# A hybrid attention and state-space block: first projections on unscaled, turned tokens

## The chip, the cores and the metric

The kernel runs on one core of a Trainium2 chip. A core has TensorE (matrix products), VectorE, ScalarE and GpSimd, SyncE which issues transfers, and 16 DMA engines. The metric is the device time of one execution in microseconds, as the median of several runs. A profile of one execution gives each instruction's start and duration.

## The reference

One decoder block on 512 tokens and 16 learned meta tokens, 1024 features, all in float32. What matters here:

```python
h = concat([meta, x])                       # 528 tokens
xn = rmsnorm(h, g_mix_pre)                  # h * rsqrt(mean(h*h) + eps) * g
proj = xn @ w_in                            # q, k, v, r, a_low, u, z_gla, z_ssm
log_a = log_sigmoid(a_low @ w_gate_up + b_gate) / 16
o = gla_chunked(q, k, v, log_a)             # gated linear attention, 4 heads
y_gla = (rmsnorm(o) * silu(r)) @ w_o_gla
y_s = s5_ssm(u, ...)                        # complex diagonal state-space layer, 64 groups
glu = gelu(y_s) @ w_glu + b_glu
y_ssm = glu[..., :1024] * sigmoid(glu[..., 1024:])
mixed = sigmoid(z_gla) * y_gla + sigmoid(z_ssm) * y_ssm
h = h + rmsnorm(mixed @ w_out, g_mix_post)
f = square(relu(rmsnorm(h, g_ffn_pre) @ w_ff1)) @ w_ff2
h = h + rmsnorm(f, g_ffn_post)              # output: the 512 tokens
```

Since rmsnorm scales each token by one number, `xn @ w` equals the product of `h * g` with `w`, scaled by that number per token afterwards.

## The kernel before

Every large product is made of three matmuls, because operands are split into a high and a low part: high x high, high x low, low x high (`mm3`). A weight tile is 1024 x 128: it is loaded into `wraw` (three buffers), ScalarE rounds it into `whi` (`split_w_hi`, three buffers), VectorE subtracts to give `wlo` (`split_w_lo`, three buffers). The activations are kept turned, features on the partitions, as `xh` and `xl`, [128, 8, 528]. A tile's product with all 528 tokens is made in two halves (`HALVES`), 256 and 272 columns; each half is 24 matmuls. A z tile is made of 24 matmuls with 512 columns.

The start: four tiles of 128 tokens and the meta tokens are loaded as rows, in `xt`. For each, ScalarE sums the squares (`squared`) and takes a root, VectorE makes the reciprocal root (`rooted`) and the normalised rows `xn` (`normed`), using `gpre`, the gain spread over the partitions by two matmuls with one row. TensorE turns `xn` in blocks of 128 x 128 (`turned_tokens`), ScalarE copies the high part to `xh` (`high`) and VectorE the low part to `xl` (`low`). Between them TensorE multiplies dummy matmuls (`busy`). Meanwhile the first three u tiles are multiplied: first halves as soon as the first 256 tokens are there, second halves behind the last. ScalarE takes each half from the accumulator into `ut` (three buffers) in another order of tokens, and GpSimd's queue stores it to DRAM (`u_out`). In this stage each engine's order is the order of the program text (`InOrder`, `keep_in_program_order`).

Behind it comes `low_rank`, the product with 16 columns of `w_in` that yields `alow`, from `xh`, `xl` and `wa`. Then a list of tiles, `dense`, is worked off by `slot()`, each with the weights of the tile fetched two ahead (`fetch`, `AHEAD = 2`): before S5's blocks, u tiles 3 to 7, four z tiles of `zs` and one of `zg`. Among these, `gate_up(h)` multiplies `alow` with `wgr` (the gate weights, split by `gate_weights` out of `wgu`, which six small loads on GpSimd's queue bring), and `decay_sums` makes the sums of log decays: exp, log and a scan for each head with a mask that restarts it at each 128 tokens. VectorE at the same time makes the state-space layer's parameters (`chain`, `powers`, `chunk_powers`, `b_bar`).

After that, eight blocks of S5, each with several `slot()` calls among its steps so that TensorE has dense work: v, q, k, the remaining z tiles, r tiles, and the o tiles. Then the GLU, the output product and the two feed-forward products. TensorE keeps program order throughout the part shown; on the other engines and queues a scheduler sets the order outside the start, and buffers' reuse adds waits.

Of the kernel before, what the change touches and what calls it, by code (L numbers as in the profile page):

```python
# [16 lines left out]
P = 128  # L17
# [3 lines left out]
NM = 16  # L21
# [28 lines left out]
def hybrid_block(ctx: ExitStack, tc: tile.TileContext, io, out: bass.AP):  # L50
# [204 lines left out]
    def u_half(w, ut, q, within=None):  # L255

        a, b = HALVES[q]
        ps = bank("mm")
        feat_tile(w, xh, xl, a, b, ps[:, : b - a], within=within)

        def taken():
            src = ps.rearrange("p (c s) -> p s c", s=T8)
            first = NM // T8 + a // T8
            S.copy(ut[:, :, first : first + 32], src[:, :, :32])
            if q:
                S.copy(ut[:, :, : NM // T8], src[:, :, 32:34])

        return taken
# [9 lines left out]
    gpre = mk(pxt, [P, D], tag="gpre")  # L278
    grow = mk(pxt, [1, D], tag="grow")
    one_row = mk(pxt, [1, P], tag="one_row")  # L280
    V.memset(one_row, 1.0)
    nc.scalar.dma_start(grow, io["g_mix_pre"][0].rearrange("(o d) -> o d", o=1))
    xm = mk(pxt, [P, D], tag="xt", bufs=5)
    xts, raws = [], []
    loaded = nc.sync.dma_start(xm[:NM], io["meta_tokens"])
    ones = mk(pxt, [P, 256], tag="ones")
    V.memset(ones, 1.0)
    idle = bank()

    def busy(n):  # L290

        for _ in range(n):
            PE.matmul(idle[:, :256], ones[:, :P], ones, start=True, stop=True)
# [3 lines left out]

    def x_load(t):
        xt = mk(pxt, [P, D], tag="xt", bufs=5)
        xts.append((xt, P, t * P))  # L300
        return nc.sync.dma_start(xt, io["x"][0, t * P : (t + 1) * P, :])


    for kind, i in (("x", 0), ("x", 1), ("u", 0), ("x", 2), ("u", 1), ("x", 3), ("u", 2)):
        with behind():
            if kind == "x":
                loaded = x_load(i)
            else:
                loaded, raw = raw_w(w_in[:, C_U + i * P : C_U + (i + 1) * P])
                raws.append(raw)  # L310
    xts.append((xm, NM, SEQ))
# [3 lines left out]
    nc.gpsimd.dma_start(vecs, io["vecs"])  # L315
    V, S = InOrder(nc.vector), InOrder(nc.scalar)
    ss = mk(pxt, [P, 5], tag="xss")
    rs = mk(pxt, [P, 5], tag="xrs")
    xns = {}

    def squared(i):
        xt, n, _ = xts[i]
        sq = mk(pxt, [P, D], tag="xsq", bufs=1)
        S.activation(sq[:n], xt[:n], AF.Square, accum_out=ss[:n, i : i + 1])

    def rooted(i):

        n = xts[i][1]
        y, ssum = rs[:n, i : i + 1], ss[:n, i : i + 1]
        parts = mk(pxt, [n, 2], tag="xr_r", bufs=3)  # L330
        a, hm = parts[:, :1], parts[:, 1:]
        S.activation(a, ssum, AF.Sqrt, scale=1.0 / D, bias=epst[:n])
        yield
        V.tensor_scalar(hm, ssum, -0.5 / D, -0.5 * EPS, op0=ALU.mult, op1=ALU.add)
        V.reciprocal(y, a)
        V.scalar_tensor_tensor(a, y, hm, y, op0=ALU.mult, op1=ALU.mult)
        V.scalar_tensor_tensor(y, a, 1.5, y, op0=ALU.add, op1=ALU.mult)

    roots = {}

    def summed(i):
        squared(i)
        roots[i] = rooted(i)
        next(roots[i])

    def normed(i, cols=(0, 512)):
        xt, n, _ = xts[i]
        if i not in xns:
            xns[i] = mk(pxt, [P, D], tag="xn", bufs=3)
            next(roots[i], None)  # L350
        xn = xns[i]
        for c in cols:
            cc = slice(c, c + 512)
            V.scalar_tensor_tensor(xn[:n, cc], xt[:n, cc], rs[:n, i : i + 1], gpre[:n, cc], op0=ALU.mult, op1=ALU.mult)

    def turned(i, tag):
        return [turned_tokens(xns[i][: xts[i][1]], xts[i][1], q, tag if isinstance(tag, str) else tag[q]) for q in range(2)]

    def high(i, q, pvs):
        _, n, col = xts[i]  # L360
        split_hi(xh[:, 4 * q : 4 * q + 4, col : col + n], pvs[q])

    def low(i, q, pvs):
        _, n, col = xts[i]
        dst = slice(4 * q, 4 * q + 4)
        V.tensor_sub(xl[:, dst, col : col + n], pvs[q], f32(xh)[:, dst, col : col + n])

    gps = [bank() for _ in range(2)]
    for i, ps in enumerate(gps):
        PE.matmul(ps, one_row, grow[:, i * 512 : (i + 1) * 512], start=True, stop=True)  # L370
# [12 lines left out]
    w0 = hi0, split_w_lo(raws[0], hi0)
    high(0, 0, t0)
    high(0, 1, t0)
    t1 = turned(1, "sm")
    high(1, 0, t1)
    high(1, 1, t1)
    for q in range(2):
        low(0, q, t0)  # L390
        low(1, q, t1)
    ut0, ut1, ut2 = (u_tile() for _ in range(3))
    take0 = u_half(w0, ut0, 0)
    summed(2)
    hi1 = split_w_hi(raws[1])
    w1 = hi1, split_w_lo(raws[1], hi1)
    take1 = u_half(w1, ut1, 0)
    normed(2)
    summed(3)
    hi2 = split_w_hi(raws[2])  # L400
    w2_ = hi2, split_w_lo(raws[2], hi2)
    take0()
    normed(3)
    ts = {}
    take2 = u_half(w2_, ut2, 0, within=(1, lambda: ts.update({2: turned(2, "mm")})))
    high(2, 0, ts[2])
    high(2, 1, ts[2])
    normed(4, (512,))
    low(2, 0, ts[2])
    low(2, 1, ts[2])  # L410
    t4 = turned(4, "sm")
    t3 = turned(3, ("mm", "sm"))
    take1()
    for q in range(2):
        high(4, q, t4)
        low(4, q, t4)
    for q in range(2):
        high(3, q, t3)
        low(3, q, t3)
    take2()  # L420
    wa = mk(pg, [P, KT, 32], F32R, tag="wa")
    split_hi(wa[:, :, :16], wraw)
    begun = V.tensor_sub(wa[:, :, 16:], wraw, f32(wa)[:, :, :16])
    V, S = nc.vector, nc.scalar
    for blk, w, ut in ((0, w0, ut0), (1, w1, ut1), (2, w2_, ut2)):
        u_half(w, ut, 1)()
        u_out(blk, ut)
# [44 lines left out]

    def gate_up(h):
        for a, b in HALVES:
            ps = bank()[:, : b - a]
            PE.matmul(ps, wgr[:, h * P : (h + 1) * P], alow[:, a:b], start=True, stop=True)
            bg = vecs[:, V_BGATE + h : V_BGATE + h + 1]
            S.activation(ga[:, h, a:b], ps, AF.Abs, bias=bg)
            V.tensor_scalar(mn[:, h, a:b], ps, bg, 0.0, op0=ALU.add, op1=ALU.min)

    def decay_sums():
        S.activation(ga, ga, AF.Exp, scale=-1.0)
        S.activation(ga, ga, AF.Ln, bias=1.0)
        for h in range(HEADS):
            V.tensor_sub(mn[:, h], mn[:, h], ga[:, h])
            b2 = mk(pga, [P, NT], tag="b2", bufs=2)
            V.tensor_tensor_scan(b2, mask01, mn[:, h], 0.0, op0=ALU.mult, op1=ALU.add)
            nc.gpsimd.dma_start(bd[h], b2)
# [21 lines left out]
    def u_slot(m):  # L510
        def go(w):
            ut = u_tile()
            for q in range(2):
                u_half(w, ut, q)()
# [219 lines left out]
    def c_rows():  # L734
        S.activation(CA, CA, AF.Copy, scale=sgn)
        S.activation(CB, CB, AF.Copy, scale=-1.0)
# [27 lines left out]
    with tc.issue_after(begun.ins):  # L764
        fetch(0)
    fetch(1)
# [44 lines left out]
    class Head:  # L811
# [27 lines left out]
        def decays(self):  # L839
# [13 lines left out]
            self.kg = ex([P, NT], dl, "gk", -1.0 / TAU)  # L853
            d1 = mk(pgb, [P, NT], tag="d1")[:, :SEQ]
            V.tensor_sub(d1.rearrange("p (c t) -> p c t", t=CH), bm, bm[:, :, 32:33].to_broadcast([P, 8, CH]))
            self.kin = ex([P, SEQ], d1, "k", -1.0 / TAU)
            self.qin = ex([P, SEQ], d1, "q", 1.0 / TAU)
            dx = mk(pgb, [P, NT], tag="d1")[:, :SEQ].rearrange("p (c t) -> p c t", t=P)
            V.tensor_sub(dx, bp, bp[:, :, 63:64].to_broadcast([P, TT, P]))
            self.kx = ex([P, TT, CH], dx[:, :, :CH], "fk", -1.0 / TAU)  # L860
            self.qx = ex([P, TT, CH], dx[:, :, CH:], "fq", 1.0 / TAU)
            self.dec = ex([P, TT], bp[:, :, P - 1], "dec", 1.0 / TAU)
            self.b2, self.ex = b2, ex

        def query_decay(self):
            self.qg = self.ex([P, SEQ], self.b2[:, :SEQ], "gq", 1.0 / TAU)
# [266 lines left out]
    for kind in ("r0", "r1", "z5", "r2", "r3", "z6", "r4", "r5", "r6", "r7", "z7", *(f"o{m}" for m in range(KT))):  # L1133
# [11 lines left out]
    for b, blk in enumerate(blocks):  # L1145
# [22 lines left out]
        slot()  # L1168
# [20 lines left out]
        slot()  # L1189
# [329 lines left out]
def laid_out(np, given):  # L1519
# [9 lines left out]
    for name, (one, two) in (("b_cols", bt), ("c_cols", ct)):  # L1529
        rows[name] = np.stack([np.concatenate([one, two]), np.concatenate([two, one])])  # L1530
    return {**{name: a[name] for name in _INS}, **rows}


_LAID = ["gla_norm_g", "b_glu", "b_gate", "d_skip", "a_re", "a_im", "log_step", "b_re", "b_im", "c_re", "c_im"]
_INS = [
    "x", "meta_tokens", "g_mix_pre", "w_in", "w_gate_up", "w_o_gla", "w_glu", "w_out", "g_mix_post", "g_ffn_pre", "w_ff1", "w_ff2", "g_ffn_post",
# [21 lines left out]
```

## Time and profile before

| | |
|---|---|
| median of 3 runs | 883.39 us (882.73 to 883.80) |
| the profiled execution | 883.62 us |
| its span | 881.9 us |
| TensorE busy | 869.5 us, 99% of the span |
| VectorE busy | 648.6 us, 74% |
| ScalarE busy | 437.7 us, 50% |
| GpSimd busy | 124.0 us, 14% |
| moved by DMA | 177.36 MB |

The rows of the profile name an engine (PE is TensorE, DVE is VectorE, ACT is ScalarE, POOL is GpSimd, SP is SyncE), the line of the program, the operation, the tile written and the tiles read, and the shape. In a timeline row the first number is the start and the second the duration in us; what stands in brackets is the idle time of that engine just before, and what ended it. In a group's row the total busy time and the mean of one in ns follow the count. TensorE's matmuls are pipelined: a row's duration is longer than the spacing of two starts. In the kernel's start all instructions behind helper `InOrder` carry line L78, and all matmuls L60, so they are told apart by their tiles.

### The profile page before, as it was taken

The numbers are of one execution on the slowest core, as the hardware profiler recorded it, in microseconds if no ns is written. First come the engines' busy times: TensorE is split into PE (matmuls) and PEld (weight loads), VectorE is DVE, ScalarE is ACT, GpSimd is POOL, SyncE is SP. The second block draws the span as 40 slices with busy tenths as digits, with TensorE's granted clock in tenths as the row PEclk, the third lists the DMA queues.
The fourth block names the chain that finished last, engine by engine and source line by source line (L and its number), as shares of the span: only waits on it lengthen the run. The fifth ranks groups of instructions, "written<-read, shape, count | busy, mean of one in ns | idle before, by whom it ended". The sixth has DMA issues, their size and how long they took to land.

```text
span 881.9 us, 13276 instructions
## 1 busy us (share of the span) xinstructions
PE 869.5 (99%) x4856; PEld 742.5 (84%) x4856; DVE 648.6 (74%) x1148; ACT 437.7 (50%) x731; POOL 124.0 (14%) x224
## 2 busy tenths in 40 slices
PE   8999999999999999999999999999999999999996
PEld 6998989898988888888888888988888888888885
DVE  7989898868778698755445765576666678788886
ACT  6475466767655454434333543333222236665763
POOL 1223022030312213232000001021112100000001
PEclk9999999999999999999999999999999999999998
DMA  9647785555454857558545761589998966856564
GB/s 305 179 126 239 205 196 143 136 134 161 109 166 126 260 130 176 170 161 274 187 143 160 228 178 57 172 288 324 333 305 298 324 244 224 280 190 194 170 209 142
DMA packets 164988, 177.36 MB, mean 201 GB/s; under 512 B 18778, under 2 KB 125306, under 8 KB 164923
## 3 DMA queue, kind: packets, MB, share of 16 engines
q1 hardware_dynamic: 146056, 114.74, 44.8%
q0 software_dynamic: 17696, 57.84, 19.4%
q10 hardware_dynamic: 1170, 3.94, 1.3%
q8 instruction: 38, 0.62, 0.3%
q14 instruction: 28, 0.22, 0.1%
HBM read 141.06 MB, written 35.42 MB: 200 GB/s over the span
## 4 chain that ended last, share of the span: by engine, by line
PE 96%; DVE 2%; ACT 1%; DMA 0%; issue 0%; DVEq 0%; SPq 0%
PE mm L60 73%; PE sm L60 21%; PE sm L65 2%; DMA xt<-in_x_dram 0%; DVE xn L78 0%; DVE wlo L78 0%; ACT xsq L78 0%; DVE c L1483 0%; DVE xl L78 0%; PE mm L65 0%; DVE ede L604 0%; DVE c L1477 0%; ACT xh L78 0%; ACT whi L78 0%; DVEq L1554 0%
## 5 line engine op out<-in xcount | busy, mean ns | idle before, releaser
L160 ACT ACTIVATE whi<-wraw 128x1024 fp32r<-128x1024 f32 x101 | 107.0, 1059 | 236.1 <-PE mm L60 207.9
L175 DVE TENSOR_TENSOR wlo<-wraw,whi 128x1024 fp32r<-128x1024 f32 x101 | 123.4, 1222 | 106.7 <-ACT whi L160 106.5
L60 PE MATMUL mm<-xh,whi 128*128 128x512 f32 (+2 forms) x544 | 182.2, 335 | 0.5 <-ACT xh L78 0.5
L60 PE MATMUL mm<-xl,whi 128*128 128x512 f32 (+2 forms) x544 | 178.6, 328 | 1.1 <-DVE xl L78 1.1
L60 PE MATMUL mm<-xh,wlo 128*128 128x512 f32 (+2 forms) x544 | 178.9, 329 | 0.2 <-DVE wlo L78 0.2
L60 PEld LDWEIGHTS mm<-xh,whi 128*128 128x128 f32 x544 | 102.7, 189 | 10.6 <-issue 1.2
L60 PEld LDWEIGHTS mm<-xl,whi 128*128 128x128 f32 x544 | 102.8, 189 | 10.0 <-DVE xl L78 1.5
L60 PEld LDWEIGHTS mm<-xh,wlo 128*128 128x128 f32 x544 | 102.6, 189 | 9.7 <-DVE wlo L78 0.6
L60 PE MATMUL mm<-hh,whi 128*128 128x512 f32 (+1 forms) x280 | 104.0, 371 | 0.0
L60 PE MATMUL mm<-hl,whi 128*128 128x512 f32 (+1 forms) x280 | 103.8, 371 | 0.0
L60 PE MATMUL mm<-hh,wlo 128*128 128x512 f32 (+1 forms) x280 | 103.8, 371 | 0.0
L1420 DVE TENSOR_TENSOR wlo<-wraw,whi 128x1024 fp32r<-128x1024 f32 x56 | 68.4, 1222 | 20.2 <-ACT whi L1416 20.0
L60 PE MATMUL sm<-wlo,fh 128*128 128x512 f32 x192 | 74.8, 390 | 0.0
L60 PE MATMUL sm<-whi,fl 128*128 128x512 f32 x192 | 74.7, 389 | 0.0
L60 PE MATMUL sm<-whi,fh 128*128 128x512 f32 x192 | 74.7, 389 | 0.0
L1416 ACT ACTIVATE whi<-wraw 128x1024 fp32r<-128x1024 f32 x56 | 58.6, 1048 | 17.2 <-PE mm L60 11.7
L60 PEld LDWEIGHTS mm<-hl,whi 128*128 128x128 f32 x280 | 52.7, 188 | 9.1
L60 PEld LDWEIGHTS mm<-hh,whi 128*128 128x128 f32 x280 | 52.7, 188 | 9.1
L60 PEld LDWEIGHTS mm<-hh,wlo 128*128 128x128 f32 x280 | 52.7, 188 | 8.9
L160 ACT ACTIVATE fh<-f 128x512 fp32r<-128x512 f32 x48 | 30.3, 631 | 45.7 <-PE sm L60 30.6
L60 PE MATMUL mm<-gh,whi 128*128 128x512 f32 x128 | 49.8, 389 | 0.0
L60 PE MATMUL mm<-gl,whi 128*128 128x512 f32 x128 | 49.8, 389 | 0.0
(415 smaller groups left out, 1635.0 us busy)
## 6 DMA issues: line engine op xcount, KB each, us to landing
wraw<-in_w_ff_dram SPq DMA_DIRECT2D x56, 512.0 KB, 4.4
wraw<-in_w_in_dram SPq DMA_DIRECT2D x48, 512.0 KB, 4.1
w2raw<-in_w_ff_dram POOLq DMA_DIRECT2D x16, 1024.0 KB, 8.5
t2d<-w2t POOLq DMA_DIRECT2D x16, 1024.0 KB, 5.8
wraw<-t2d SPq DMA_DIRECT2D x32, 512.0 KB, 3.8
wraw<-in_w_glu_dram SPq DMA_DIRECT2D x16, 512.0 KB, 4.4
M<-kpad POOLq DMA_DIRECT2D x64, 64.0 KB, 2.6
wraw<-in_w_o_gla_dram SPq DMA_DIRECT2D x8, 512.0 KB, 7.9
```

The source lines that it names most:

```text
L60: ins = nc.tensor.matmul(*args, **kw)
L65: ins = nc.tensor.transpose(*args, **kw)
L160: S.activation(dst, src, AF.Copy, scale=scale)
L175: V.tensor_sub(lo, raw, f32(hi))
L1416: halved = S.activation(bh, raw, AF.Copy)
L1420: V.tensor_sub(bl, raw, f32(bh))
```

## The change

1. The host lays the tokens out turned as well: `x_cols0` (first 256 tokens) and `x_cols1` (the other 256 and the meta tokens), and the gain as `g_cols`, one column for each feature group. `xT` is loaded from them.
2. u tiles 0 to 4 are multiplied with unscaled tokens: `rh`, `rl` are the high and low part of x times g, made by ScalarE and VectorE for each of eight slices and both halves. The token's scale is applied when the product is taken from the accumulator, on VectorE (`u_took(..., raw=True)` multiplies with `rowp`), where before ScalarE copied.
3. The token scales are found in two groups from the x rows (still loaded, three buffers, squares in place), and five small matmuls spread them over the partitions (`spread`). ScalarE writes them to `rows` and, in the other token order, `rowp`.
4. x is normalised in turned form behind that: `scaled` (VectorE), `high` (ScalarE), `low` (VectorE). The 40 transposes and the two matmuls that spread the gain are gone; five dummy matmuls stand at the start.
5. `gate_up`: the minimum is taken by ScalarE (`Relu` with the sign turned), and the following subtraction goes into the scan, which runs in five pieces for each head, without a mask. Signs in the exponents turn accordingly.
6. `dense`: u tiles 5 to 7, four `zs` and three `zg` tiles (before: five u, four and one). z5 and z6 leave the r phase and go through DRAM; two slots in the last S5 block are skipped.
7. The first three fetches stand together behind the start, the scaling of C's rows (`c_rows`) as well.

```diff
+    scale_rows = []
+    def u_took(ps, ut, q, raw=False):
+        a = HALVES[q][0]
+        src = ps.rearrange("p (c s) -> p s c", s=T8)
...
+            if raw:
+                V.tensor_mul(dst, got, scale_rows[0][:, :, to : to + n])
+            else:
+                S.copy(dst, got)
...
+    for k in range(0, KT, 2):
+        with behind():
+            loaded = nc.sync.dma_start(xT[:, k : k + 2, :256], io["x_cols0"][:, k : k + 2])
...
+    for kind, i in (("u", 1), ("h", 0), ("h", 4), ("u", 2), ("x", 0), ("x", 1), ("x", 2), ("x", 3), ("x", 4), ("u", 3), ("u", 4)):
...
+    def taken_raw(k, q):
+        g, cols = g8[:, k : k + 1], slice(*HALVES[q])
+        S.activation(rh[:, k, cols], xT[:, k, cols], AF.Copy, scale=g)
+        V.scalar_tensor_tensor(rl[:, k, cols], xT[:, k, cols], g, f32(rh)[:, k, cols], op0=ALU.mult, op1=ALU.subtract)
...
+    def spread(q):
+        ps = bank()
+        for j, i in enumerate(range(3 * q, 3 * q + 2) if not q else range(2, TT + 1)):
+            n = xts[i][1]
+            PE.matmul(ps[:, j * P : j * P + n], rs[:n, i : i + 1].to_broadcast([n, P]), ident[:n, :n], start=True, stop=True)
+        return ps
...
+    def scaled(q, ks):
+        cols = slice(*HALVES[q])
+        for k in ks:
+            V.scalar_tensor_tensor(xT[:, k, cols], xT[:, k, cols], g8[:, k : k + 1], rows[:, cols], op0=ALU.mult, op1=ALU.mult)
+    def high(q, ks):
...
+            S.copy(xh[:, k, cols], xT[:, k, cols])
+    def low(q, ks):
...
+            V.tensor_sub(xl[:, kk, cols], xT[:, kk, cols], f32(xh)[:, kk, cols])
...
+    uts = [u_tile() for _ in range(3)]
+    busy(5)
...
+    raw_product(w0, 0, pair)
...
+    raw_product(w1, 0, pair[:, 256:])
+    for k in range(KT):
+        taken_raw(k, 1)
+    raw_product(w0, 1, last[0])
+    raw_product(w1, 1, last[1])
+    w2_ = split_w(raws[2])
+    squared(0)
+    squared(1)
+    rooted(slice(0, 2))
+    squared(2)
+    ps = spread(0)
+    rows_of(0, ps)
+    raw_product(w2_, 0, pair2)
+    for i in range(2):
+        u_took(pair[:, 256 * i : 256 * i + 256], uts[i], 0, True)
...
+    raw_product(w4, 0, last[4])
+    uts.extend(u_tile() for _ in range(2))
+    u_took(pair2[:, 256:], uts[3], 0, True)
+    for k in range(0, KT, 2):
+        scaled(1, (k, k + 1))
+        high(1, (k, k + 1))
+        if k:
+            low(1, (k - 2,))
+    low(1, (KT - 2,))
+    raw_product(w4, 1, last[5])
+    begun_s = S.activation(wa[:, :, :16], wraw, AF.Copy)
+    begun = V.tensor_sub(wa[:, :, 16:], wraw, f32(wa)[:, :, :16])
+    u_took(last[3], uts[3], 1, True)
...
             S.activation(ga[:, h, a:b], ps, AF.Abs, bias=bg)
-            V.tensor_scalar(mn[:, h, a:b], ps, bg, 0.0, op0=ALU.add, op1=ALU.min)
+            S.activation(mn[:, h, a:b], ps, AF.Relu, bias=nbg[:, h : h + 1], scale=-1.0)
...
-            V.tensor_sub(mn[:, h], mn[:, h], ga[:, h])
-            V.tensor_tensor_scan(b2, mask01, mn[:, h], 0.0, op0=ALU.mult, op1=ALU.add)
+            for c in range(0, NT, P):
+                cc = slice(c, min(c + P, NT))
+                V.tensor_tensor_scan(b2[:, cc], mn[:, h, cc], ga[:, h, cc], 0.0, op0=ALU.add, op1=ALU.add)
...
-    for m in range(3, KT):
+    for m in range(5, KT):
         u_slot(m)
     for m in range(4):
         gate_slot(C_ZS, m, zs, early_tile)
-    gate_slot(C_ZG, 4, zg, early_tile)
+    for m in range(4, 7):
+        gate_slot(C_ZG, m, zg, early_tile)
...
-    with tc.issue_after(begun.ins):
-        fetch(0)
-    fetch(1)
+    with tc.issue_after(begun.ins), tc.issue_after(begun_s.ins):
+        for i in range(AHEAD + 1):
+            fetch(i)
...
-    for kind in ("r0", "r1", "z5", "r2", "r3", "z6", "r4", "r5", "r6", "r7", "z7", *(f"o{m}" for m in range(KT))):
+    for kind in ("r0", "r1", "r2", "r3", "r4", "r5", "r6", "r7", "z7", *(f"o{m}" for m in range(KT))):
...
-        slot()
+        if b < NBLK - 1:
+            slot()
```

More of the change, by code (lines that the diff above doesn't have):

```diff
@@ L277, in hybrid_block, with busy @@
     pxt = pool("pxt", stack=sx, padded=True)
[L278 to L285, printed above, removed]
     ones = mk(pxt, [P, 256], tag="ones")
     V.memset(ones, 1.0)
[L288 to L293, printed above, removed]
+    g8 = mk(pxt, [P, KT], tag="g8")
+    nc.scalar.dma_start(g8, io["g_cols"])
+    xT = mk(pxt, [P, KT, NT], tag="xT")
+    rh, rl = (mk(pxt, [P, KT, LINE + SEQ], F32R, tag=t)[:, :, :NT] for t in ("rh", "rl"))
+    raws, xts, loaded = [mk(wp, [P, KT, P], tag="wraw", bufs=3)], {}, None
     def behind():
         return tc.issue_after(loaded.ins) if loaded else ExitStack()
-    def x_load(t):
[L299 to L304, printed above, removed]
+    for k in range(0, KT, 2):
+        with behind():
+            loaded = nc.sync.dma_start(xT[:, k : k + 2, :256], io["x_cols0"][:, k : k + 2])
+        if k % 4 == 0:
+            with behind():
+                loaded = nc.sync.dma_start(raws[0][:, k : k + 4], w_in[k * P : (k + 4) * P, C_U : C_U + P].rearrange("(k p) n -> p k n", p=P))
+    idle = bank()
+    def busy(n, cols=256):
+        for _ in range(n):
+            PE.matmul(idle[:, :cols], ones[:, :P], ones[:, :cols], start=True, stop=True)
+    def x_load(t):
+        n = NM if t == TT else P
+        xt = mk(pxt, [P, D], tag="xt", bufs=3)
+        xts[t] = xt, n
+        return nc.sync.dma_start(xt[:n], io["meta_tokens"] if t == TT else io["x"][0, t * P : (t + 1) * P, :])
+    for kind, i in (("u", 1), ("h", 0), ("h", 4), ("u", 2), ("x", 0), ("x", 1), ("x", 2), ("x", 3), ("x", 4), ("u", 3), ("u", 4)):
         with behind():
@@ L321, in squared @@
     def squared(i):
[L322 to L334, printed above, removed]
+        xt, n = xts[i]
@@ L335, in rooted @@
+        S.activation(xt[:n], xt[:n], AF.Square, accum_out=ss[:n, i : i + 1])
+    def rooted(c):
+        y, ms = rs[:, c], ss[:, c]
+        n = c.stop - c.start
+        a, hm = (mk(pxt, [P, n], tag=f"{t}{n}") for t in ("xra", "xrh"))
+        S.activation(a, ms, AF.Sqrt, scale=1.0 / D, bias=epst)
+        V.tensor_scalar(hm, ms, -0.5 / D, -0.5 * EPS, op0=ALU.mult, op1=ALU.add)
         V.reciprocal(y, a)
-        V.scalar_tensor_tensor(a, y, hm, y, op0=ALU.mult, op1=ALU.mult)
+        V.tensor_mul(a, y, y)
+        V.tensor_mul(a, a, hm)
@@ L356, in turned @@
[L356 to L370, printed above, removed]
@@ L393, in hybrid_block @@
[L393 to L411, printed above, removed]
@@ L412, in hybrid_block @@
[L412 to L423, printed above, removed]
+    rowp = scale_rows[0]
+    def spread(q):
[4 more added lines that the diff above has]
+        return ps
@@ new lines, in hybrid_block @@
+    last = {0: bank("mm"), 1: bank("mm")}
+    raw_product(w0, 1, last[0])
[7 more added lines that the diff above has]
+    rows_of(0, ps)
+    pair2 = bank("mm")
+    raw_product(w2_, 0, pair2)
+    for i in range(2):
+        u_took(pair[:, 256 * i : 256 * i + 256], uts[i], 0, True)
+    squared(3)
+    scaled(0, range(0, 4))
+    w3 = split_w(raws[3])
+    squared(4)
+    high(0, range(0, 4))
@@ new lines, in hybrid_block @@
+    rooted(slice(2, TT + 1))
+    scaled(0, range(4, 8))
+    low(0, (0, 2))
+    last[2] = bank("mm")
+    raw_product(w2_, 1, last[2])
+    ps = spread(1)
+    raw_product(w3, 0, pair2[:, 256:])
+    high(0, range(4, 8))
+    rows_of(1, ps)
+    w4 = split_w(raws[4])
+    low(0, (4, 6))
+    for i in range(2):
+        u_took(last[i], uts[i], 1, True)
+        u_out(i, uts[i])
+    last[3] = bank()
+    raw_product(w3, 1, last[3])
+    u_took(pair2[:, :256], uts[2], 0, True)
+    u_took(last[2], uts[2], 1, True)
```

136 lines of the change are left out of this document (68 added, 68 removed).

## The prediction, made before the changed kernel was run

> **What bounds the kernel now.** I read the page first: engine totals and the chain that ended last.
>
> ```profile
> span 881.9 us, 13276 instructions
> PE 869.5 (99%) x4856; PEld 742.5 (84%) x4856; DVE 648.6 (74%) x1148; ACT 437.7 (50%) x731; POOL 124.0 (14%) x224
> PE 96%; DVE 2%; ACT 1%; DMA 0%; issue 0%; DVEq 0%; SPq 0%
> ```
>
> TensorE is busy in 869.5 of 881.9 us and carries 96% of the chain. Nothing is won by lighter VectorE or ScalarE work unless it closes a hole in TensorE's queue, so the second view is the busy time by stage, to find the 12.4 us of holes.
>
> ```profile
> 25.00:30.00 5.00, 4.02 (x32) 3.54 (x32) 4.86 (x18) 2.00 (x6) 2.92 (x6) 1.00 0.36 98
> 30.00:35.00 5.00, 5.00 (x42) 5.00 (x42) 5.00 (x34) 2.62 (x6) 1.09 (x2) 1.00 0.25 68
> 35.00:40.00 5.00, 5.00 (x43) 4.52 (x43) 4.09 (x15) 2.35 (x7) 1.12 (x2) 1.00 0.92 256
> 870.00:875.00 5.00, 4.18 (x19) 3.13 (x17) 2.70 (x9) 1.73 (x6) 0.37 (x1) 1.00 0.00 0
> 875.00:880.00 5.00, 0.00 (x0) 0.00 (x0) 2.61 (x8) 0.23 (x1) 0.69 (x2) 0.62 0.67 202
> ```
>
> The columns after the stretch are its length, then TensorE, weight loads, VectorE, ScalarE, GpSimd, the granted clock, DMA share and GB/s. From 30 us on TensorE is full. It ends at 874.18 (870 + 4.18), so 7.7 us of the holes are the tail, which the change does not touch; the rest lies before 30 us. So only the start can give time: its holes, and the TensorE work there that is no part of the answer. Third view, TensorE's timeline:
>
> ```profile
> 2.65 3.75 PE L60 MATMUL sm<-grow,one_row 1*128 1x512 f32 x4 [2.65 <-DMA grow<-in_g_mix_pre_dram]
> 6.33 2.08 PE L60 MATMUL sm<-ones 128*128 128x256 f32 x4
> 8.58 1.94 PE L65 MATMUL mm<-ident,xn 128*128 128x128 f32 x8 [0.18 <-DVE xn L78]
> 12.02 1.32 PE L65 MATMUL sm<-ident,xn 128*128 128x128 f32 x8
> 13.60 0.38 PE L60 MATMUL mm<-xh,whi 128*128 128x256 f32 x1 [0.25 <-ACT xh L78]
> 14.66 0.29 PE L60 MATMUL mm<-xh,whi 128*128 128x256 f32 x1
> 17.30 0.28 PE L60 MATMUL mm<-xl,whi 128*128 128x256 f32 x1
> 21.17 1.03 PE L65 MATMUL mm<-ident,xn 128*128 128x128 f32 x8
> 28.05 0.30 PE L60 MATMUL mm<-xh,whi 128*128 128x272 f32 x1
> 36.58 0.28 PE L60 MATMUL mm<-xh,wlo 128*128 128x272 f32 x1
> 36.70 0.28 PE L60 MATMUL mm<-xh,wa 128*32 128x256 f32 x1
> ```
>
> Until 13.60 TensorE spreads the gain, runs dummies and transposes. Products are spaced 0.12 us at 256 columns (22 from 14.66 to 17.30) and 0.125 at 272 (69 from 28.05 to 36.70). So one u tile is 24 x 0.12 + 24 x 0.125 = 5.89 us. Three are done at 36.70, when low_rank begins: 17.7 us of product, 19.0 us of everything else.
>
> **The change, the start.** The yardstick is the start of low_rank with five u tiles done. Before that would be 36.70 + 2 x 5.89 = 48.5. For the changed kernel I walked the four queues by hand, with these durations (line groups; busy total and mean ns of one):
>
> ```profile
> L78 ACT ACTIVATE whi<-wraw 128x1024 fp32r<-128x1024 f32 x3 | 3.1, 1042 | 0.0
> L78 ACT ACTIVATE xsq<-xt 128x1024 f32<-128x1024 f32 x4 | 4.2, 1054 | 1.2 <-DMA xt<-in_x_dram 1.2
> L78 ACT ACTIVATE xh<-mm 128x512 fp32r<-128x512 f32 x5 | 2.9, 597 | 2.5 <-PE mm L65 2.5
> L264 ACT COPY ut<-mm 128x256 f32<-128x256 f32 x7 | 2.5, 360 | 0.1
> L78 DVE TENSOR_TENSOR wlo<-wraw,whi 128x1024 fp32r<-128x1024 f32 x3 | 3.7, 1220 | 0.9 <-ACT whi L78 0.9
> L78 DVE SCALAR_TENSOR_TENSOR xn<-xt,xrs,gpre 128x512 f32<-128x512 f32 x8 | 5.6, 746 | 0.1
> L78 DVE TENSOR_TENSOR xl<-mm,xh 128x512 fp32r<-128x512 f32 x5 | 3.3, 677 | 0.0
> L219 DVE TENSOR_TENSOR lp4a<-lamp 128x256 f32<-128x256 f32 x1 | 0.4, 418 | 0.0
> xt<-in_x_dram SPq DMA_DIRECT2D x4, 512.0 KB, 7.2
> ud<-ut POOLq DMA_DIRECT2D x5, 264.0 KB, 3.2
> 5.53 1.06 ACT L78 ACTIVATE xsq<-xt 128x1024 f32<-128x1024 f32 x1 [1.15 <-DMA xt<-in_x_dram]
> ```
>
> Instructions that follow each other overlap by some 0.08 us, so in a full queue I charge 0.60 for a 512-column pass on VectorE, 1.14 for 1024, 0.34 for 256. A scalar_tensor_tensor at 512 costs 0.07 more than a plain pass (746 against 677), so one at 256 is put at 0.40.
>
> First data: the first 0.58 MB (meta tokens and one x tile) are there at 5.53, 4 KB at 2.65. The new first piece, 0.26 MB, I put between them in proportion to its size, at 4.0; the next five pieces follow at the rate of 0.58 MB minus 0.26 in 1.5 us or somewhat faster, one each 0.7 us, to 7.6. The first half of u0 is paced by them and ends near 9.9; the first half of u1 begins at 10.4. From there TensorE has its work back to back: u1's first half and two second halves 8.9 us (to 19.3), two spreading matmuls 0.4, u2 5.9, three spreading matmuls and a short wait 0.8, u3 and u4 11.8: the last raw product ends at **38.1**.
>
> That does not start low_rank, since it needs x normalised, and VectorE makes that last. Its queue up to the low part of wa, in order of kind: 16 low parts of the raw tokens 6.4 us, low parts of five weight tiles 6.1, 16 scaled slices 6.4, eight low passes of 512 or 544 columns 5.0, scaled evictions of seven half tiles 2.8, roots and wa 1.2: 27.9 us of work. Its waits: 4.4 until the first piece has passed ScalarE, 1.2 for later pieces, 2.0 for the squares (x as rows is loaded behind 3.7 MB of other data), 1.9 for the row scale to go through TensorE and ScalarE, 1.0 at the second root, 0.9 for u4's weights, and 2.2 at u3's first eviction: it writes the buffer that u0 leaves (three ut buffers), so it waits for u0's store, 3.2 us from an issue at about 32. Sum 13.6. So low_rank starts at 27.9 + 13.6 = 41.5 by kinds, **41.7** in the walk with its rounding: 48.5 - 41.7 = **6.8 us gained**, and a hole of 3.6 us in TensorE ahead of it. With a store of 2.6 us and earlier data it is 41.0; with x tiles landing as late as the 7.2 of the row makes possible, 43.4. Bounds of the gain: 5.1 to 7.5; if VectorE did not wait at its buffer and TensorE ran straight on, 10.4.
>
> **The gates' weights.** Here I expect part of it back. gate_up(0) stands in TensorE's queue right behind u5. On ScalarE, wgr's split (in gate_weights) now stands behind the whi split of the fourth fetched tile, and that one reuses u5's whi buffer, so it waits for u5's last matmul. On VectorE the same tile's wlo stands ahead of wgr's low part.
>
> ```profile
> L160 ACT ACTIVATE wgr<-wgu 96x512 fp32r<-96x512 f32 x1 | 0.6, 632 | 1.7 <-DMA wgu<-in_w_gate_up_dram 1.7
> L456 DVE TENSOR_TENSOR wgr<-wgu,wgr 32x512 fp32r<-32x512 f32 x1 | 0.7, 683 | 0.8 <-ACT wgr L160 0.8
> L479 DVE TENSOR_SCALAR mn<-sm,vecs 128x272 f32<-128x272 f32 x4 | 2.0, 490 | 0.0
> L487 DVE TENSOR_TENSOR_SCAN b<-mask,mn 128x528 f32<-128x528 f32 x4 | 5.0, 1242 | 0.0
> ```
>
> From u5's last matmul: whi 1.04, then wlo 1.14 on VectorE (wgr's 0.63 on ScalarE runs beside it), then wgr's low part 0.68: gate_up(0) starts 2.85 us late, and everything behind it on TensorE with it. That was free before: wgr waited only for its DMA (1.7) and was ready long ahead. **Minus 2.85**; bounds 1.5 (the order costs less but wgu's six loads on GpSimd's queue, now behind more stores, land that late) and 3.5.
>
> **The rest.** Minimum on ScalarE: eight passes of about 0.49 leave VectorE (3.9 us), four subtractions too; eight of the same size come to ScalarE, which is at half load (50%). The scan in five pieces costs four starts more for each head; I put that at nothing to 2 us in all, on VectorE. TensorE waited for neither from 30 us on, so I take 0. The fifth z tile ahead of S5 has its wlo behind the scans and the powers of E8 on VectorE's queue; I take 0, as z tiles before had no wait, with 1.5 as the other end. z5 and z6 leave the r phase, so r tiles come closer together:
>
> ```profile
> 334.32:366.57 32.25, 32.25 (x189) 26.75 (x188) 30.06 (x49) 15.86 (x28) 7.19 (x13) 1.00 0.63 168
> 366.57:398.82 32.25, 32.25 (x189) 26.75 (x188) 16.66 (x23) 9.94 (x16) 10.02 (x18) 1.00 0.59 172
> ```
>
> The first stretch, one block's six slots with four r tiles, has VectorE at 30.06 of 32.25 and TensorE without a hole; a fifth r tile in such a stretch brings it to about 31.9. I take 0, the other end is 2 us. The last block loses two covering slots, but VectorE is half idle there (16.66): 0. TensorE's total in the slots is the same.
>
> **The clock.** Two holes of 3.6 and 2.85 us are new, and a hole may cost more than itself. In the tail the granted clock is 0.62 over 875 to 880. If it falls to 0.5, it was full for 1.2 us, to 876.2: it fell 2.0 us after the last matmul. On the other side 1 us of holes between 25 and 30 (4.02 busy) left it at 1.00. At the start eight transposes take 1.94 at 8.58, 1.32 at 12.02 and 1.03 when warm: half rate until about 12.6 although dense work ran from 6.33, so 6.3 us. A fall therefore costs from nothing to 6.3 / 2 = 3.15 us; I take half, 1.6, and one fall, at the wider hole. [...]
>
> **The sum.** 6.8 - 2.85 - 0 - 1.6 = 2.3 us. The profiled execution took 883.62 (span 881.9 and 1.7 around it), the median is 883.39, so they agree: 883.4 - 2.3 = **881.1**. A difference under 0.2% (1.8 us) is what a measurement of this kernel can hardly tell from none.
>
> **The rivals.**
> *The clock holds (faster).* Neither hole lowers it; for: the 1 us of holes between 25 and 30 us did no harm; against: the tail. Gain 6.8 - 2.85 = 3.9, so 879.5; with the first hole halved as well (store 2.6 us, VectorE less late) 5.7, so 877.7, and with nothing behind low_rank lost 875. [...]
> *The clock falls twice and stays down (slower).* Both holes lower it, and each time it takes 6.3 us of dense matmuls to come back, as at the start: 6.3 us lost, 6.8 - 2.85 - 6.3 = -2.4, so 885.8. It decides from 7.9 us at half rate on (3.9 gained, at half a microsecond for each). For: both holes exceed 2.0 us. Against: the start was the chip's first work, and the first 3.75 us of it were one-row matmuls.
> *VectorE becomes the bound in the r phase or the z stage.* 1.5 and 2.0 us of waits on top: 881.1 + 3.5 = 884.6. For: 31.9 of 32.25. Against: lighter scans and gates ahead of it.
> *The start does not get earlier.* The loads to u4's weights are 6.95 MB, 2.2 more than before, because x is loaded twice. If they, not VectorE, set the pace and the last lands some 5 us later than walked, the gain falls to about 2 and the 2.85 eats it: 884.2.
>
> **How the numbers follow.** Forecast case 0.40 (its own range 879.5 to 884: faster 0.23, same 0.14, slower 0.03); clock holds 0.25 (all faster); two long falls 0.20 (slower); VectorE later on 0.10 (same 0.03, slower 0.07); loads 0.05 (same 0.02, slower 0.03). Faster 0.48, same 0.19, slower 0.33. The range takes in the first rival's far end and the second's with 1.2 us of z wait: 875 to 887.
>
> **What would show it.** Right: first useful matmul near 5.5, raw products done near 38, low_rank near 41.7 behind VectorE, gate_up 2.85 us behind u5 on wgr. A fall shows as 0.24 us instead of 0.12 between products in the 6 us after each hole. Wrong: low_rank under 40 or over 44, gate_up without a wait, or TensorE waits past 80 us.

## The result, and the profile after

The changed kernel takes 892.98 us (median of 4 runs, 889.8 to 893.94) against 883.06: a ratio of 1.0108, 95% interval 1.0079 to 1.0137. It is slower by about 9.9 us; the forecast was 2.3 us faster, with a range that ended at 887. The page of the changed kernel, lines as shown of before:

```profile
span 891.8 us, 13281 instructions
PE 870.5 (98%) x4824; PEld 744.1 (83%) x4824; DVE 651.7 (73%) x1180; ACT 445.6 (50%) x751; POOL 125.3 (14%) x220
PE 90%; ACT 3%; DMA 2%; DVE 2%; issue 1%; SPq 0%; POOL 0%; DVEq 0%; ACTq 0%; POOLq 0%
```

TensorE has fewer instructions (4824 against 4856) and yet is busy 1.0 us longer, in a span that is 9.9 us longer; its share of the chain fell from 96% to 90%. So there are new holes, and some of what runs takes longer. What TensorE waited for, in all, times, longest:

```profile
PE mm L60 <- DVE wa L78: 4.4, 1, 4.4
PE mm L60 <- DVE wlo L175: 3.1, 1, 3.1
PE sm L60 <- DVE wgr L498: 3.0, 1, 3.0
PE sm L60 <- DVE xrs L78: 1.5, 1, 1.5
PE sm L60 <- DVE xss L331: 1.3, 1, 1.3
```

Where these holes lie, on TensorE's timeline:

```profile
5.89 0.58 PE L60 MATMUL mm<-rh,whi 128*128 128x256 f32 x1
44.50 0.28 PE L60 MATMUL mm<-xh,wa 128*32 128x256 f32 x1 [4.40 <-DVE wa L78]
59.00 0.58 PE L60 MATMUL sm<-alow,wgr 96*128 96x256 f32 x1 [3.04 <-DVE wgr L498]
100.15 0.79 PE L60 MATMUL mm<-xh,wlo 128*128 128x512 f32 x1 [3.09 <-DVE wlo L175]
```

The first useful matmul starts at 5.89 instead of 13.60, and the raw products end at 40.1. low_rank starts at 44.50; with five u tiles before's yardstick was 48.5. The start thus gave 4.0 us. The other two holes, ahead of gate_up(0) and within the fifth z tile, take 6.1 us back. What is left of the loss I look for in the clock. The busy time by stretches, cut at the granted clock's changes (columns as in the prediction; the clock is the third from the end):

```profile
41.52:44.93 3.41, 0.43 (x4) 0.40 (x5) 3.41 (x9) 2.78 (x6) 0.00 (x0) 1.00 0.00 0
44.93:48.34 3.41, 3.41 (x18) 2.49 (x17) 3.40 (x8) 2.11 (x5) 3.07 (x5) 0.50 0.70 189
48.34:51.76 3.42, 3.42 (x30) 3.14 (x29) 2.51 (x6) 2.86 (x5) 3.42 (x7) 1.00 0.99 316
55.17:58.58 3.41, 0.79 (x7) 0.56 (x5) 2.17 (x6) 1.90 (x4) 0.47 (x1) 1.00 0.57 144
58.58:62.00 3.42, 3.00 (x14) 3.00 (x15) 3.04 (x15) 2.38 (x7) 0.09 (x1) 0.50 0.67 200
62.00:65.41 3.41, 3.41 (x18) 3.41 (x18) 3.41 (x29) 0.70 (x3) 0.00 (x0) 0.50 0.13 37
96.13:99.54 3.41, 0.93 (x5) 0.43 (x3) 3.41 (x9) 1.26 (x3) 1.08 (x3) 1.00 0.52 168
99.54:102.96 3.42, 2.81 (x7) 2.23 (x8) 3.42 (x5) 2.13 (x5) 2.13 (x4) 0.50 0.82 202
102.96:106.37 3.41, 3.41 (x10) 2.63 (x9) 3.41 (x6) 0.00 (x0) 0.00 (x0) 0.50 0.76 187
106.37:109.78 3.41, 3.41 (x16) 2.77 (x15) 2.94 (x4) 0.47 (x1) 0.00 (x0) 1.00 1.12 327
```

After each hole the clock is at one half, for one or two stretches of 3.41 us. How much slower the products are there is read from the spacing of their starts:

```profile
60.05 0.41 PE L60 MATMUL mm<-xh,whi 128*128 128x256 f32 x1
62.18 0.41 PE L60 MATMUL mm<-xl,whi 128*128 128x256 f32 x1
100.74 0.63 PE L60 MATMUL mm<-xh,whi 128*128 128x512 f32 x1
105.86 0.63 PE L60 MATMUL mm<-xh,whi 128*128 128x512 f32 x1
```

From the first row to the second there are ten spacings, 0.213 us each, against 0.12 at full clock; from the third to the fourth twelve, of 512 columns, 0.427 each, against 0.227 (nine from 94.63 to 96.67). So 44% and 47% of the busy time at half clock is lost, a little less than half: 0.44 x (3.41 + 3.00 + 3.41) + 0.47 x (2.81 + 3.41) = 7.2 us. The last run below (e9) has the same 4564 matmuls from low_rank on, and no stretch at half clock among them. Compared with it start by start, the three falls cost 1.5, 2.9 and 3.0 us, **7.4** in all, and each of the two holes 0.16 us beyond its length: the first product behind the third hole is followed after 0.59 us (100.15 to 100.74), the next ones after 0.43. The account: 4.0 - 3.04 - 3.09 - 7.4 - 0.3 = -9.8; the spans differ by 9.9.

The causes of the three holes on VectorE's and ScalarE's timelines:

```profile
33.32 1.66 DVE L78 TENSOR_TENSOR ut<-mm,xrowp 128x256 f32<-128x256 f32 x7
37.89 0.42 DVE L78 TENSOR_TENSOR ut<-mm,xrowp 128x256 f32<-128x256 f32 x1 [2.92 <-DMA ud<-ut]
44.08 0.28 DVE L78 TENSOR_TENSOR wa<-waraw,wa 128x128 fp32r<-128x128 f32 x1
57.00 1.23 DVE L175 TENSOR_TENSOR wlo<-wraw,whi 128x1024 fp32r<-128x1024 f32 x1
58.26 0.68 DVE L498 TENSOR_TENSOR wgr<-wgu,wgr 32x512 fp32r<-32x512 f32 x1
98.16 0.82 DVE L533 TENSOR_TENSOR_SCAN b<-mn,ga 128x128 f32<-128x128 f32 x3
98.89 1.20 DVE L175 TENSOR_TENSOR wlo<-wraw,whi 128x1024 fp32r<-128x1024 f32 x1
```

```profile
55.91 1.06 ACT L160 ACTIVATE whi<-wraw 128x1024 fp32r<-128x1024 f32 x1 [2.56 <-PE mm L60]
56.88 0.61 ACT L160 ACTIVATE wgr<-wgu 96x512 fp32r<-96x512 f32 x1
```

VectorE waits 2.92 us for u0's store before it can write u3's first half, and finishes wa only at 44.4. wgr stands behind whi and wlo of another tile, as forecast. The fifth z tile's wlo stands behind the last scans and the powers between them.

The theory to test: these three places in the queues, and the clock that falls behind them, are the whole loss; the rest of the change costs nothing. The rival: the loss sits in what follows (the denser r phase, VectorE, the doubled x loads), and the holes only show it.

### The profile page after: what moved, and what is told of

It reads as the page before. It is cut to its first block, busy times and chain, and to the rows that moved or that the text cites. A ratio compares the mean times of both kernels' runs of the same rounds, so it can differ in the third digit from the quotient of the medians.

```text
span 891.8 us, 13281 instructions
## 1 busy us (share of the span) xinstructions
PE 870.5 (98%) x4824; PEld 744.1 (83%) x4824; DVE 651.7 (73%) x1180; ACT 445.6 (50%) x751; POOL 125.3 (14%) x220
## 4 chain that ended last, share of the span: by engine, by line
PE 90%; ACT 3%; DMA 2%; DVE 2%; issue 1%; SPq 0%; POOL 0%; DVEq 0%; ACTq 0%; POOLq 0%
PE mm L60 67%; PE sm L60 21%; PE sm L65 2%; DMA xT<-in_x_cols_dram 1%; DMA bd<-b 1%; DMA wraw<-in_w_in_dram 1%; DVE xT L78 0%; DMA ud<-ut 0%; ACT rh L78 0%; ACT xt L78 0%; DVE xl L78 0%; ACT xh L78 0%; ACT whi L160 0%; ACT whi L78 0%; DVE c L1533 0%
## 5 line engine op out<-in xcount | busy, mean ns | idle before, releaser
L160 ACT ACTIVATE whi<-wraw 128x1024 fp32r<-128x1024 f32 x99 | 104.6, 1059 | 234.6 <-PE mm L60 208.1
L175 DVE TENSOR_TENSOR wlo<-wraw,whi 128x1024 fp32r<-128x1024 f32 x99 | 121.0, 1222 | 104.1 <-ACT whi L160 103.7
L60 PE MATMUL mm<-xh,wlo 128*128 128x512 f32 (+2 forms) x464 | 158.3, 341 | 3.1 <-DVE wlo L175 3.1
L60 PE MATMUL mm<-xh,whi 128*128 128x512 f32 (+2 forms) x464 | 161.3, 348 | 0.0
L60 PE MATMUL mm<-xl,whi 128*128 128x512 f32 (+2 forms) x464 | 157.7, 340 | 0.0
L60 PEld LDWEIGHTS mm<-xh,wlo 128*128 128x128 f32 x464 | 89.3, 192 | 12.9 <-DVE wlo L175 3.5
L60 PEld LDWEIGHTS mm<-xh,whi 128*128 128x128 f32 x464 | 89.6, 193 | 9.8 <-issue 1.2
L60 PEld LDWEIGHTS mm<-xl,whi 128*128 128x128 f32 x464 | 89.6, 193 | 8.8
L1470 DVE TENSOR_TENSOR wlo<-wraw,whi 128x1024 fp32r<-128x1024 f32 x56 | 68.4, 1222 | 19.7 <-ACT whi L1466 19.5
L1466 ACT ACTIVATE whi<-wraw 128x1024 fp32r<-128x1024 f32 x56 | 58.6, 1049 | 17.0 <-PE mm L60 11.7
L160 ACT ACTIVATE fh<-f 128x512 fp32r<-128x512 f32 x48 | 30.3, 631 | 45.5 <-PE sm L60 30.4
```

The source lines that it names most:

```text
L60: ins = nc.tensor.matmul(*args, **kw)
L160: S.activation(dst, src, AF.Copy, scale=scale)
L175: V.tensor_sub(lo, raw, f32(hi))
L1466: halved = S.activation(bh, raw, AF.Copy)
L1470: V.tensor_sub(bl, raw, f32(bh))
```

## The experiments

### Filling the holes

```diff
     raw_product(w4, 1, last[5])
+    busy(16)
...
     slot()
+    filler(26)          # 26 matmuls of ident with ident, 128 columns
     gate_up(0)
...
         next(first, None)
+        if i == 1:
+            filler(26)
         slot()
```

> The three holes of the changed kernel (4.4 us ahead of low_rank, 3.0 us ahead of gate_up(0), 3.1 us ahead of the fifth z tile) are filled with matmuls that nobody reads: 16 of 256 columns, 26 and 26 of 128, about 3.7, 2.8 and 2.8 us at full clock. They are a little shorter than the holes, so nothing useful starts later than it would. Theory (holes lower the clock, and the clock costs more than the holes do): the half-rate stretches, 3.4, 6.2 and 5.5 us long with work in them, go, which gives back half of each, 7.6 us: about 885.4 us, between 884 and 887, granted clock 1.00 in all stages from 15 us to the tail. Rival (the clock is not what costs, the loss sits in later waits of VectorE or DMA): 892 to 894, no change.

Measured: 897.95 us (ratio 1.0169, 1.0154 to 1.0184), outside both forecasts. The clock was 1.00 in every stretch from 35 us to the tail, but the filling was mis-sized: each dummy shows as two rows of the trace, and they took about twice what I had charged (7.07 us for 3.7, 5.97 for 2.8).

```profile
40.42 7.07 PE L60 MATMUL sm<-ones 128*128 128x256 f32 x32
57.05 5.97 PE L60 MATMUL sm<-ident 128*128 128x128 f32 x52
```

So this run shows only that the clock stayed at 1.00 with TensorE at work; it says nothing on the price. Repeated with 9, 13 and 13:

> As the first filling, with the matmuls counted by what they took there at full clock (0.44 us for 256 columns, 0.23 for 128): 9, 13 and 13, so 4.0, 3.0 and 3.0 us for holes of 4.4, 3.0 and 3.1. Theory (the holes lower the clock): no half-rate stretch is left, 7.6 us come back: 885.4 us, between 884.5 and 887. Rival (the clock's loss was made up for elsewhere, or the holes are set by PE's own delays and move along): 890 or more.

```profile
40.22 4.05 PE L60 MATMUL sm<-ones 128*128 128x256 f32 x18
45.52 0.31 PE L60 MATMUL mm<-xh,wa 128*32 128x256 f32 x1 [1.25 <-DVE wa L78]
55.28 3.06 PE L60 MATMUL sm<-ident 128*128 128x128 f32 x26
58.94 0.76 PE L60 MATMUL sm<-alow,wgr 96*128 96x256 f32 x4 [0.60 <-DVE wgr L499]
```

Measured: 888.38 us (887.31 to 889.08). Useless work of the holes' length makes the kernel 4.6 us faster, with the clock at 1.00 up to the tail. That is short of the forecast of 7.6. The clock cost 7.4 us (above), but in this run low_rank came 1.0 us later than in the changed kernel, gate_up waited 0.6 us on top of its filling, 0.65 us went around 420 us, where TensorE waited for `gl` (0.2 us by the list of waits), and the tail was 0.4 us longer. The holes are as long as before, filled instead of empty, and yet 4.6 of the 9.9 us come back; so the clock costs about half of the loss at least, and the rival of the first run (no change) is not left.

### Each hole by itself

The gates' weights ahead of the fourth fetched tile:

```diff
+            if n == 3:
+                with tc.issue_after(gw[0].ins), tc.issue_after(gw[1].ins):   # wgr's two instructions
+                    ready[n] = load_w(dense[n][0])[0]
```

> Only the issue order of the gates' weights changes: the split of the fourth fetched tile is queued behind wgr's two instructions on ScalarE and VectorE instead of ahead of them. Theory: the 3.0 us hole ahead of gate_up(0) closes and with it the half-rate stretch behind it (3.1 us): 893.0 - 6.1 = 886.9, between 885.5 and 888.5. Rival one (the six small loads of wgu land too late anyway): the hole shrinks only to 1.5 or 2 us, at most 1.5 us faster. Rival two (the fourth tile's weights become late instead): the hole moves to the fourth tile, time within 1.5 us of 893.

Measured: 887.4 us (886.34 to 887.79), 5.6 faster. What is left of the wait, in this kernel's list and on ScalarE:

```profile
PE sm L60 <- DVE wgr L498: 0.6, 1, 0.6
57.11 0.63 ACT L497 ACTIVATE wgr<-wgu 96x512 fp32r<-96x512 f32 x1 [1.80 <-DMA wgu<-in_w_gate_up_dram]
```

The hole is 0.6 instead of 3.0 us and no clock falls behind it. Now it is wgu's loads that end last, so rival one holds in small. That the total agrees with the forecast of 6.1 is in part luck, for the other two places moved as well: low_rank started at 45.3 instead of 44.5 (its wait is 4.9 in the list), the fall there lasted two stretches instead of one, and the hole in the fifth z tile shrank to 1.8 us with a fall of one stretch instead of two.

Own buffers for u0's and u1's output:

```diff
-    uts = [u_tile() for _ in range(3)]
+    uts = [mk(pxt, [P, T8, NCK], tag="utx", bufs=2) for _ in range(2)] + [u_tile()]
```

> u0 and u1 get output buffers of their own, so that u3's first eviction does not wait on VectorE for u0's store (2.9 us). Theory: VectorE reaches wa 2.9 us earlier, low_rank starts near 41.6 instead of 44.5 us, the hole ahead of it shrinks from 4.4 to 1.5 us and no longer lowers the clock (1.7 us): 893.0 - 4.6 = 888.4, between 887 and 890; the other two holes stay. Rival: another wait on VectorE takes the place of this one (a late accumulator or late slices), hole over 2 us, the clock still falls: gain under 2 us.

Measured: 887.38 us (887.19 to 888.51), 5.6 faster. TensorE's timeline, list of waits, a row of VectorE, and stretches:

```profile
41.80 0.28 PE L60 MATMUL mm<-xh,wa 128*32 128x256 f32 x1 [1.30 <-DVE wa L78]
PE sm L60 <- DVE wgr L498: 4.5, 1, 4.5
PE mm L60 <- DVE wlo L175: 3.1, 1, 3.1
53.55 0.20 DVE L633 TENSOR_SCALAR ab<-ab 128x64 f32<-128x64 f32 x1 [4.77 <-DMA ab<-in_a_step_dram]
92.17:95.59 3.42, 1.55 (x7) 0.94 (x5) 3.27 (x10) 0.64 (x3) 1.39 (x3) 1.00 0.53 186
95.59:99.00 3.41, 2.18 (x9) 1.80 (x10) 3.41 (x5) 2.74 (x5) 2.40 (x4) 1.00 0.72 201
99.00:102.41 3.41, 3.41 (x16) 2.82 (x15) 3.41 (x4) 0.00 (x0) 0.00 (x0) 1.00 0.86 143
```

low_rank is at 41.80 as expected, with a hole of 1.3 us and no fall. The total is in the range for a reason that the forecast did not have: gate_up's hole grew to 4.5, with a fall of 2.4 us behind it, but the third hole, still 3.1 us, no longer lowers the clock. It now straddles two stretches, with 1.55 and 2.18 us of work in them; in the changed kernel the same hole left 0.93 in one. gate_up's hole grew because VectorE stood until 53.55 at an instruction that waits for another small load, `ab`, behind wgu's on GpSimd's queue; wlo and wgr's low part are queued behind it, 1.4 us after whi was ready.

The scans of heads 2 and 3 behind the fifth z tile's wlo:

```diff
+            if h == 2:
+                fetch(7)
+            with tc.issue_after(los[-1].ins) if h >= 2 else ExitStack():
                 for c in range(0, NT, P):
```

> The scans of heads 2 and 3 are queued on VectorE behind the low part of the fifth z tile's weights. Theory: the 3.1 us hole ahead of that tile closes, and the half-rate stretch behind it (2.8 us): 893.0 - 5.9 = 887.1, between 885.5 and 889; the first two holes stay. Rival one: the low part is then held up by its own high part or its load, hole over 1.5 us. Rival two: the decays of the first head come late and the hole turns up in the first S5 block: time within 1.5 us of 893.

Measured: 887.6 us (887.32 to 888.01), 5.4 faster. For this edit the tile is fetched ahead of those scans. The low part ran early, and TensorE's list has no such wait any more:

```profile
92.23 1.22 DVE L177 TENSOR_TENSOR wlo<-wraw,whi 128x1024 fp32r<-128x1024 f32 x1
```

Nothing turned up in the first S5 block. The first two holes stayed (4.7 and 3.0 us), but their falls changed places in length: two stretches at low_rank (45.3 us here), one behind gate_up.

### The minimum back on VectorE

```diff
-            S.activation(mn[:, h, a:b], ps, AF.Relu, bias=nbg[:, h : h + 1], scale=-1.0)
+            V.tensor_scalar(mn[:, h, a:b], ps, bg, 0.0, op0=ALU.add, op1=ALU.min)
```

> The changed kernel with the gates' minimum back on VectorE (eight passes of 0.48 us) and a scan that subtracts; all else as changed. Theory (this part only moves load between engines that are not the bound; the order of the queues makes the holes): the first two holes stay at 4.4 and 3.0 us, the third grows by up to 2 us, as VectorE gets 3.9 us more and ScalarE's exponentials come earlier by at most as much: 891 to 896. Rival (the minimum on ScalarE is what made the third hole, by delaying the logarithm): the third hole closes, 887.

Measured: 893.6 us (892.56 to 893.82): no change beside 892.98. The list of waits:

```profile
PE mm L60 <- DVE wa L78: 4.8, 1, 4.8
PE mm L60 <- DVE wlo L175: 3.3, 1, 3.3
PE sm L60 <- DVE wgr L498: 3.1, 1, 3.1
```

The three holes are within 0.4 us of what they were. In this run the logarithm ended at 78.3 us (76.37 + 1.97) instead of 87.2, and the third hole is still there. Together with the run that moved the scans, that leaves the low part's place in VectorE's queue as its cause, not the minimum and not a late logarithm.

### All three together

The three edits, and the loads of wgu at the start, into memory that the start does not use.

> The three corrections together (own output buffers for u0 and u1, gate weights split ahead of the fourth tile, scans of heads 2 and 3 behind the fifth z tile's weights), and the six loads of wgu issued at the start into memory of their own, since with an earlier low_rank they land too late. Theory: low_rank starts near 41.6 us instead of 48.5 (the kernel before, with five tiles done) and no hole over 1.5 us is left behind it: 883.2 - 6.9 = 876.3, between 875 and 878.5. Rival one: a hole turns up at another tile behind gate_up or in the first S5 block, 2 to 4 us: 879 to 881. Rival two: the unscaled start has a cost in the S5 blocks that the holes hid: 883 or more.

Measured: 878.31 us (877.75 to 878.55), ratio 0.9943 (0.9928 to 0.9958): faster than both kernels. It is 2.0 us short of the forecast, mostly because low_rank starts at 42.7 instead of 41.6. There is no wait over 0.5 us behind low_rank. Two stretches of its profile:

```profile
26.81:30.22 3.41, 1.82 (x14) 1.55 (x13) 2.41 (x9) 2.18 (x8) 0.00 (x0) 1.00 1.02 382
30.22:33.64 3.42, 3.42 (x19) 3.42 (x18) 2.56 (x4) 1.86 (x5) 0.00 (x0) 0.50 0.82 248
```

The 1.6 us hole ahead of the second spreading had fallen into one stretch, and the clock fell behind it. I filled it (run e8), and in a second run (e9) also held wgu's loads back:

```diff
+    busy(3)
     ps = spread(1)
```

> The version with the three corrections, and three matmuls that nobody reads (1.3 us) in the 1.6 us hole ahead of the second spreading of the row scale. In that version's trace the clock fell for 3.4 us behind this hole. Theory (a window of 3.41 us with about 1.6 us or more without matmuls lowers the clock for one or two such windows): the hole is now 0.3 us, the clock stays, 1.7 us come back: 878.3 - 1.7 = 876.6, between 875.8 and 877.4. Rival (the fall there was of one execution only, the median has none): 878.3 within 0.6.

> As e8, with the six loads of wgu held until the first row scale is found (near 19 us), since with them at the very start VectorE's chain ran 1.1 us later than in the changed kernel as delivered (second reciprocal at 27.70 against 26.56 us). Theory (they take transfer time from the first x and weight pieces): low_rank about 1.1 us earlier, 875.5, between 874.7 and 876.5. Rival (the 1.1 us have another cause, or the end of low_rank's chain does not move): as e8 within 0.4.

Measured: 878.12 us (877.46 to 878.68) and 877.67 us (877.18 to 879.75; ratio 0.994, 0.9927 to 0.9952). low_rank, filled and held:

```profile
42.66 0.30 PE L60 MATMUL mm<-xh,wa 128*32 128x256 f32 x1 [1.32 <-DVE wa L78]
```

```profile
41.75 0.30 PE L60 MATMUL mm<-xh,wa 128*32 128x256 f32 x1 [1.33 <-DVE wa L78]
```

In the first, the clock held (a mean of 0.998, against 0.996) and nothing was won. What was saved on raw products came back as the 1.32 us wait, since VectorE sets low_rank's start; the half-rate work ahead of it had cost nothing. I had not seen this when I wrote the expectation. In the second, low_rank came 0.9 us earlier, as the theory had it, but the median moved by 0.45 only, within the two runs' spread, so the gain in time stays open.

### The account over all runs

For each profiled execution: span, less low_rank's start, less the holes and useless work behind it, less what the half clock cost behind it (each matmul's start against e9's).

| kernel | span | low_rank at | holes behind | clock | rest |
|---|---|---|---|---|---|
| before (five u tiles) | 881.9 | 48.5 | 0 | 0 | 833.4 |
| changed | 891.8 | 44.5 | 6.1 | 7.4 | 833.8 |
| gates' weights first | 885.9 | 45.3 | 2.4 | 4.2 | 834.0 |
| own output buffers | 885.6 | 41.8 | 7.6 | 2.4 | 833.8 |
| scans behind | 886.3 | 45.3 | 3.0 | 4.0 | 834.0 |
| minimum on VectorE | 890.7 | 45.3 | 6.3 | 5.5 | 833.6 |
| short filling | 886.7 | 45.5 | 6.7 | 0 | 834.5 |
| all closed | 876.5 | 42.7 | 0.5 | 0 | 833.3 |
| and filled spread | 876.4 | 42.7 | 0.3 | 0 | 833.4 |
| and wgu held | 875.5 | 41.8 | 0.3 | 0 | 833.4 |

The rest is the same to 0.7 us in all but the short filling. From 146 us to its last matmul the changed kernel keeps its distance to e9, start by start, within 0.05 us: nothing of its loss arises there. And e9's rest, with the same r phase, last block, scan in pieces and doubled x loads, is that of the kernel before. Taken together these parts cost nothing that can be seen, and the rival falls; a cost of one hidden by a gain of another is not excluded.

## Why the prediction was wrong

**The bound: right.** Only TensorE's queue counted, and the start gave time.

**The start: right in mechanism, mis-sized.** 4.0 us instead of 6.8. VectorE did set low_rank, and the wait at u3's buffer was there, but VectorE reached that point at 35.0 rather than near 33, and the store landed 3.7 us after its issue at 34.12 rather than 3.2 after 32. Up to there VectorE's first pass began at 5.17 instead of 4.4; it waited 0.83 us at 24.11 for the fourth weight tile, which the sum of waits doesn't have; and the two roots with wa took some 2.0 us, not 1.2. One reading in the working was wrong: 0.58 MB minus 0.26 in 1.5 us makes 1.2 us for a piece of 0.26 MB, not 0.7; ScalarE's first passes over the pieces began at 4.62, 6.10, 7.22 and 8.33. From the store to the end of wa it took 6.5 us, as walked. The measured gain lies under the lower bound that I had given (5.1).

**The gates' weights: right.** 3.04 us against 2.85, by the queue order that the prediction named.

**The fifth z tile: a term put at 0 that was 3.1.** The prediction named the place (wlo behind scans and powers of E8) and took 0, because z tiles before had no wait, with 1.5 as the end. It measured 3.09. A row from a kernel in which the tile stood two slots further from the scans was no measure of it.

**The clock: the step that decided.** I charged one fall of 1.6 us; there were three, of 1.5, 2.9 and 3.0 us, 7.4 in all. The rows that I had were right on the fall (the tail: 2.0 us of idle time) and I still let two of three events out: one as too short, one because I had set its hole to 0. No fall cost more than the bound of 3.15, and two of the three came near it. But the 6.3 us that it was made of were read from the lengths of transposes alone (1.94 and 1.32 against 1.03); the clock column of before is 1.00 from 0 to 15 us, so a half clock at the start was not shown. That the first cost 1.5, close to the 1.6 charged, is luck: it was half of a bound, and what made it small is that its half rate lasted one stretch and not two. The rival with two long falls, 885.8, was the nearest, with a chance of 0.20; it lacked the z hole of 3.1 and its fall of 3.0, and 2.8 less from the start, and it charged the first fall 1.6 too much.

Between the forecast (2.3 us faster) and the account (9.8 slower) lie 12.1 us: 5.8 from the clock, 3.1 from the z hole, 2.8 from the start, 0.2 from the gates' weights and 0.3 from the 0.16 beyond the length of each of two holes (the sum differs by rounding).

All half-rate stretches ahead of the tail are one or two times 3.41 us long, and TensorE was not idle in the 3.41 us ahead of a fall: 0.79, 0.93 and even 1.82 us of busy time there still ended in one.

**The rest: right as a sum.** r phase, last block, scans and the minimum were put at 0, and the account leaves nothing for them; only the minimum was tried by itself.

## What to carry to other kernels

In a kernel whose TensorE is 99% busy, a hole of 2 to 5 us cost itself and, in these runs, nothing to 3 us of clock behind it (1.5, 2.9 and 3.0 behind holes of 4.4, 3.0 and 3.1 in the changed kernel, none behind 3.1 with the own output buffers), so price a new wait at up to twice its length, and look for what stands ahead of the needed instruction on its own queue. Four edits of queue order, buffers and load order, which touch no arithmetic, turned 9.9 us of loss into 5 us of gain. Before filling a hole with useless work, ask whether the next thing is set by another engine: here, work at half clock ahead of such a wait cost nothing (878.31 us with it, 878.12 without).

## What the runs showed of the hardware

Every fall ahead of the tail, in all profiled executions, lasted 3.41 or 6.83 us. When a hole began did not set when the clock fell: in the changed kernel it fell 4.8, 2.6 and 2.5 us after the holes began, at 44.93, 58.58 and 99.54 us, and these points lie 4 and 12 times 3.41 us apart. What a hole of 3.1 us did differed with how such stretches cut it: the clock fell where one stretch kept 0.93 us of work, and did not where two kept 1.55 and 2.18. Behind holes of 1.8 us (gates' weights first, 1.60 us of busy time in the stretch) and 1.6 us (all closed, 1.82) it fell too. Busy time of 1.55 without a fall and 1.82 with one are the wrong way round for a threshold on busy time, also for the 1.6 us without matmuls that the expectation of e8 took: 1.87 us without busy time in a stretch (3.42 less 1.55) didn't lower the clock. But the busy time is the length of rows that run past the next start (0.39 us against 0.227 at 512 columns): by columns, the stretch of 1.55 had more work, six matmuls of 512, against six of 256 and spreads of 272 columns in all in the stretch of 1.82. What in a stretch decides was not shown.

A second stretch at half rate mostly followed where the hole reached into the first, as at 58.58 (by 0.42 us) and 99.54 (by 0.61). Not always: with the minimum on VectorE the hole ahead of low_rank reached 0.5 us into the half-rate stretch at 44.75, and the clock was back after that one stretch.

The changed kernel's four runs spread from 889.8 to 893.94 us, while before's lie between 881.6 and 883.8. Their order is that of the granted clock: spans of 888.1, 890.8, 891.8 and 892.2 us at a mean clock of 0.991, 0.990, 0.988 and 0.986. A clock lower by 0.005 over 890 us is 4.5 us of full clock, and the spans differ by 4.1. So the spread goes with the clock; why the clock differs from run to run, the unprofiled runs don't show.
